# Second layer norm with TensorE's order written down and half its groups made affine ahead of the transpose; another unit order in the second half of the down product; the first norm's first product by parts

## The chip, the cores and the metric

The kernel runs on one core of one Trainium2 chip. The time is the device time of one execution in microseconds; it is given as the median of several runs. The engines are TensorE (PE, with its weight loads PEld), VectorE (DVE), ScalarE (ACT), GpSimd (POOL) and SyncE (SP), which here only issues transfers.

## What is computed

One decoder block on 256 tokens of width 2048, in float32:

```python
x = layer_norm(ALPHA * x + mix, ln1_g[i], ln1_b[i])       # mix: two token mixers, gated, times w_out
ffn = conv_gated_mlp(x, w_gate[i], w_up[i], conv_w[i], conv_b[i], w_down[i])   # 2048 -> 5632 -> 2048
x = layer_norm(ALPHA * x + ffn, ln2_g[i], ln2_b[i])
x = x + jax.nn.sigmoid(x @ w_ple_gate[i]) * (p[i] @ w_ple_proj[i])
```

The stages of the program, in order of time, are the mixers with their projections, the product `wo` with `w_out`, the first layer norm, the gate and up products (44 column groups), the down product in two halves of 1024 output columns, the second layer norm, and the last product `pg` with `w_ple_gate`, whose sigmoid is multiplied with the small projection `pp`.

## The kernel before

**Weights.** Nearly all weights come as units of 128 x 2048 numbers (1 MB), in the order in which they are used. `prep` (L133) fetches a unit in two transfers `raw` from SP's queue and splits it: ScalarE writes the rounded part `hi` (`copy`, L83), VectorE the rest `lo` (L146). A product is then hi x hi + lo x hi + hi x lo. `unit` takes the next unit and prepares up to two ahead. There are four buffers for `raw` and six each for `hi` and `lo`. SP's order is the program's.

**Down product.** Each half (`down`, from L1086) goes over 22 pairs of 128-row groups, one unit a pair, in the order `DN_ORDER`. Fifteen pairs are classic: 24 matmuls, two tiles each of `hi` and `lo`. Seven pairs (`DN_S`) are done with Strassen's seven products: 21 matmuls, but VectorE forms four differences `T` (L127) and splits six tiles (L107, L121). After the last Strassen pair `fold` adds the products up in `z`. The second half holds its last two pairs back as a tail: for each token half `t` and each 512 columns `c` their 12 matmuls are done, and `ev` adds the result to `z` and takes the statistics of these 512 columns (L1144, L1145). A token's four groups `g` of 512 columns are the units of the norm.

**Layer norm.** From the statistics VectorE, GpSimd (the power -1/2) and VectorE again make the mean and the scale. In the second norm (`ln_out`, from L762) each group is then normed (g 0 on VectorE, L774; the others on ScalarE, L777), transposed on TensorE into a bank `ptl` (L780; four transposes of 128 x 128), scaled by gain and bias per channel in four operations on ScalarE and VectorE (L787, L789), and split into the parts of `x2T`. The first norm (`ln_steps`, from L795) does its groups 0 and 2 (`AFF_DVE`) otherwise: two VectorE operations of 512 columns norm them and apply gain and bias (L814, L816) ahead of the transpose, and the transposed bank is split at once (`split_T`, L712). Two banks hold turned groups. What the transposed path leaves undone in `z` itself is done later by `affine` (L862, L864), pulled in between units of the product that follows.

**What sets the order.** A scheduler orders each engine's instructions by priority and its own estimate of when they can run. SP is in program order, and in `end1`, after the product `wo`, so is TensorE: there the turns of the first norm stand between the last quarters of `wo`, the projection `pp` (`proj`) and the first three gate and up products (`psg0`, `psu0`, `psg1`). These three are first done for the first token half (`phase0`, 16 small matmuls each) and then for the second (`phase1`, a group at a time). In the second norm the scheduler sets TensorE's order.

Of the kernel before, what the change touches and what calls it, by code (L numbers as in the profile page):

```python
# [19 lines left out]
P = 128  # L20
# [21 lines left out]
DN_ORDER = (0, 1, 2, 3, 4, 5, 7, 6, 8, 10, 9, 13, 11, 12, 16, 14, 19, 15, 17, 18, 20, 21)  # L42
ZN_DVE = (0,)
# [9 lines left out]
def tile_block(ctx: ExitStack, tc: tile.TileContext, wu, wfv, wpp, xT_in, x_in, pT_in, wlr,  # L53
# [38 lines left out]
    for _ in range(9):  # L92
# [6 lines left out]
    dn_s = {dn0 + nh * (NF // 2) + i for nh in range(2) for i, n in enumerate(DN_ORDER)  # L99
            if n in DN_S}  # L100
# [167 lines left out]
    def x_half(name, act, K, evac, pulls=0, head=0, tail=0, mid=None, done=None, end=None,  # L268
               fine=False):
# [13 lines left out]
        us = [unit() for _ in range(head)]  # L283
        for t in range(2):
            for i, w in enumerate(us):
                mm(i, w, (t,))
        for i in range(head, n - tail):
# [14 lines left out]
        for t in range(2):  # L302
            for c in range(2):
                bs = banks[t][c]
                for j, ps in enumerate(bs):
                    for i, w in enumerate(us):
                        mm(n - tail + i, w, (t,), (c,), j)
                    if len(bs) == 1:
                        evac(t, c, ps)
                    else:  # L310
                        evac(t, c, ps[:, 0:256], (256 * j, 256 * j + 256))
            if done is not None:
                done(t)
# [448 lines left out]
    def ln_out(zof, stats, t, act_out, cg, cb, nm, prio):  # L762

        mv = sm.tile([P, 8], F32, tag="mv", name="mv")
        with tc.high_priority(P_STAT):
            nc.vector.bn_aggr(mv[:, 0:2], stats[t])
            nc.vector.tensor_scalar(mv[:, 2:3], mv[:, 1:2], LN_EPS, None, ALU.add)
            nc.gpsimd.tensor_tensor(mv[:, 3:4], mv[:, 2:3], mhalf, ALU.pow)
            nc.vector.tensor_scalar(mv[:, 4:5], mv[:, 0:1], -1.0, mv[:, 3:4], ALU.mult, ALU.mult)
        with tc.high_priority(prio):  # L770
            for g in range(4):
                zc = zof(t, g)
                if g in ZN_DVE:
                    nc.vector.tensor_scalar(zc, zc, mv[:, 0:1], mv[:, 3:4], ALU.subtract,  # L774
                                            ALU.mult)
                else:
                    nc.scalar.activation(zc, zc, AF.Identity, scale=mv[:, 3:4], bias=mv[:, 4:5])  # L777
                pt = mxtile(f"pt{nm}{t}{g}")
                for i in range(4):
                    nc.tensor.transpose(pt[:, i * P:i * P + P], zc[:, i * P:i * P + P], ident)  # L780
                y = t2("lny").rearrange("p (k t) -> p k t", t=P)
                for i in range(4):
                    kt = 4 * g + i
                    gc, bc = chn[:, cg + kt:cg + kt + 1], chn[:, cb + kt:cb + kt + 1]
                    src = pt[:, i * P:i * P + P]
                    if i % 2:
                        nc.scalar.activation(y[:, i, :], src, AF.Identity, scale=gc, bias=bc)  # L787
                    else:
                        nc.vector.tensor_scalar(y[:, i, :], src, gc, bc, ALU.mult, ALU.add)  # L789
                hi = act_out[g][:, :, t * P:t * P + P]  # L790
                copy(hi, y)
                nc.vector.tensor_tensor(act_out[g][:, :, 256 + t * P:256 + t * P + P], y,
                                        hi.bitcast(F32), ALU.subtract)

    def ln_steps(zs, stats, t, act_out, gb_, cg, cb, nm):  # L795


        z = zs[t]
# [10 lines left out]
        def norm(g):  # L809
            e = slice(g * 512, g * 512 + 512)  # L810
            zc = z[:, e]
            with tc.high_priority(P_LN1[t]):
# [8 lines left out]
        def turn(g):  # L821
            zc = z[:, g * 512:g * 512 + 512]
            with tc.high_priority(P_LN1[t]):
# [22 lines left out]
    def residual(name, act, K, zs, stats, mid, done=None, end=None):  # L846

        for nh in range(2):
            def ev(t, c, ps, nh=nh):
                g = 2 * nh + c  # L850
                zc = zs[t][:, g * 512:g * 512 + 512]
                with tc.high_priority(P_STAT):
# [3 lines left out]
                   done=done if nh == 1 else None, end=end if nh == 1 else None)  # L856

    def affine(zof, gb_, after, gs=range(4)):
        for t in range(2):
            for g in gs:  # L860
                zc = zof(t, g)
                nc.vector.tensor_tensor(zc, zc, gb_[0][:, g * 512:g * 512 + 512], ALU.mult)  # L862
# [40 lines left out]

    def mid1():
        for t in range(2):
            nc.sync.dma_start(z1[t], x_in[t])
        gain[0] = load_gain(0)
# [4 lines left out]
    def end1(tail_mm):  # L912
# [3 lines left out]
        with tc.manual_schedule(engines={mybir.EngineType.PE}):  # L916
# [16 lines left out]
            def phase0(i):  # L933
                us.append(unit())
                ps.append(mmtile(("psg0", "psu0", "psg1")[i]))
                w_phase(ps[i], *us[i], x1T, 0, kts)
# [9 lines left out]
            stat0, norm0, turn0 = ln_steps(z1, st1, 0, x1T, gain[0], c_g1, c_b1, "l1")  # L946
            stat1, norm1, turn1 = ln_steps(z1, st1, 1, x1T, gain[0], c_g1, c_b1, "l1")
# [15 lines left out]
            turn0(G[3])  # L963
# [19 lines left out]
    mixers.append(affine(lambda t, g: z1[t][:, g * 512:g * 512 + 512], gain[0], lambda t: nc.gpsimd.dma_start(x1d[t], z1[t]),  # L983
# [95 lines left out]
    def done2(t):  # L1079
        if t == 1:  # L1080
            pb.extend(ple_proj(1, *pq[0]))
        else:
            x2T.extend(s8([P, 4, 512], F32R, name=f"x2T{g}") for g in range(4))
        ln_out(z2of, st2, t, x2T, c_g2, c_b2, "l2", P_LN2[t])

    def down(nh, tail, mid):  # L1086
# [59 lines left out]

        n = len(DN_ORDER)
        for i, pair in enumerate(DN_ORDER[:n - tail]):
# [3 lines left out]
            if pair == DN_S[-1]:  # L1152
                fold()
        us = [unit() for _ in range(tail)]
        for t in range(2):
            for c in range(2):
                for pair, w in zip(DN_ORDER[n - tail:], us):
                    classic(pair, w, (t,), (c,))
                ev(t, c)
            if tail:  # L1160
                done2(t)
# [6 lines left out]
    down(1, 2, {6: lambda: load_z2(1), 11: late_loads, 17: lambda: pq.append(ple_prep(1))})  # L1168
# [4 lines left out]
    mixers.append(affine(z2of, gain[1], lambda t: None))  # L1173
# [7 lines left out]
    for nh in range(2):  # L1181
# [12 lines left out]
        x_half(f"pg{nh}", x2T, 16, ev_o, pulls=3, head=2 if nh == 0 else 0,  # L1194
# [21 lines left out]
def _dst(w):  # L1216

    out = []
    for nh in range(2):
        for n in DN_ORDER:  # L1220
# [76 lines left out]
```

## Time and profile before

| | us |
|---|---|
| median of 3 runs (lowest, highest) | 1709.33 (1708.78, 1711.75) |
| the profiled execution, its own time | 1707.28 |
| its span | 1705.4 |
| TensorE busy | 1691.5 |
| VectorE busy | 1174.7 |
| ScalarE busy | 862.5 |
| TensorE idle within 857 to 873 (first norm) | 1.05 + 1.65 |
| TensorE idle within 1594 to 1598 (second norm) | 3.14 |

In the rows of the profile an instruction has its line in the kernel, its engine, what it writes and reads by the program's names, and shapes (partitions x columns). "Idle before" is how long the engine did nothing just before, and what ended that. A stretch of time is given in us from the span's start. The granted clock is the share of TensorE's full clock. A matmul's row is longer than its distance from the next, since matmuls overlap.

### The profile page before, as it was taken

The numbers are of one execution on the slowest core, as the hardware profiler recorded it, in microseconds if no ns is written. First come the engines' busy times: TensorE is split into PE (matmuls) and PEld (weight loads), VectorE is DVE, ScalarE is ACT, GpSimd is POOL, SyncE is SP. The second block draws the span as 40 slices with busy tenths as digits, with TensorE's granted clock in tenths as the row PEclk, the third lists the DMA queues.
The fourth block names the chain that finished last, engine by engine and source line by source line (L and its number), as shares of the span: only waits on it lengthen the run. The fifth ranks groups of instructions, "written<-read, shape, count | busy, mean of one in ns | idle before, by whom it ended". The sixth has DMA issues, their size and how long they took to land.

```text
span 1705.4 us, 24004 instructions
## 1 busy us (share of the span) xinstructions
PE 1691.5 (99%) x8993; PEld 1447.4 (85%) x8993; DVE 1174.7 (69%) x1751; ACT 862.5 (51%) x1265; POOL 39.4 (2%) x123
## 2 busy tenths in 40 slices
PE   9999999999999999999999999999999999999998
PEld 8888888888888888888788888888888877878787
DVE  6666658658756557774687677666666887877864
ACT  5745445445555544443365555444444555455633
POOL 0000000000000000000010000000000000000000
PEclk9999999999999999999999999999999999999999
DMA  9654455555555555557665555555555555567454
GB/s 313 229 188 166 164 185 174 177 178 175 174 176 170 168 189 187 189 191 277 214 207 201 186 191 191 186 187 190 192 186 188 171 199 195 197 210 277 162 180 166
DMA packets 91717, 330.24 MB, mean 194 GB/s; under 512 B 10264, under 2 KB 11936, under 8 KB 90448
## 3 DMA queue, kind: packets, MB, share of 16 engines
q1 hardware_dynamic: 90816, 324.51, 56.2%
q0 software_dynamic: 784, 4.20, 0.7%
q8 instruction: 70, 1.15, 0.3%
q14 instruction: 47, 0.39, 0.1%
HBM read 323.42 MB, written 5.25 MB: 193 GB/s over the span
## 4 chain that ended last, share of the span: by engine, by line
PE 93%; DVE 3%; DMA 2%; ACT 1%; issue 1%; SPq 0%; POOL 0%; ACTq 0%; DVEq 0%
PE dn L1106 10%; PE psu L210 9%; PE psg L210 9%; PE psm L210 7%; PE gr L254 5%; PE gv L254 5%; PE psu L212 5%; PE psg L212 5%; PE pg L254 4%; PE psm L212 4%; PE psa L210 3%; PE wo L254 3%; PE fv L361 2%; PE dn_p L1106 2%; DMA raw<-in_wu_dram 2%; PE psa L212 2%
## 5 line engine op out<-in xcount | busy, mean ns | idle before, releaser
L146 DVE TENSOR_TENSOR lo<-raw,hi 128x1024 fp32r<-128x1024 f32 x540 | 658.1, 1223 | 407.0 <-ACT hi L83 405.8
L83 ACT ACTIVATE hi<-raw 128x1024 fp32r<-128x1024 f32 x554 | 585.6, 1059 | 644.4 <-issue 253.2
L210 PE MATMUL psu<-x1T,hi 128*128 128x512 f32 x688 | 242.2, 394 | 0.0
L210 PE MATMUL psg<-x1T,hi 128*128 128x512 f32 x672 | 236.5, 393 | 0.0
L212 PE MATMUL psu<-x1T,lo 128*128 128x256 f32 x688 | 192.6, 280 | 0.0
L212 PE MATMUL psg<-x1T,lo 128*128 128x256 f32 x672 | 188.1, 280 | 0.0
L210 PE MATMUL psm<-xT,hi 128*128 128x512 f32 x512 | 180.1, 395 | 0.0
L210 PEld LDWEIGHTS psu<-x1T,hi 128*128 128x128 f32 x688 | 129.4, 188 | 29.5
L210 PEld LDWEIGHTS psg<-x1T,hi 128*128 128x128 f32 x672 | 126.4, 188 | 28.9
L212 PE MATMUL psm<-xT,lo 128*128 128x256 f32 x512 | 143.3, 280 | 0.0
L1106 PE MATMUL dn<-hi,hC 128*128 128x512 f32 x480 | 135.8, 397 | 0.0
L212 PEld LDWEIGHTS psu<-x1T,lo 128*128 128x128 f32 x688 | 129.4, 188 | 0.0
L212 PEld LDWEIGHTS psg<-x1T,lo 128*128 128x128 f32 x672 | 126.4, 188 | 0.0
L210 PEld LDWEIGHTS psm<-xT,hi 128*128 128x128 f32 x512 | 96.2, 188 | 21.6
L1106 PEld LDWEIGHTS dn<-hi,hC 128*128 128x128 f32 x480 | 90.9, 189 | 21.5
L212 PEld LDWEIGHTS psm<-xT,lo 128*128 128x128 f32 x512 | 96.5, 188 | 0.2
L210 PE MATMUL psa<-oT,hi 128*128 128x512 f32 x256 | 90.1, 393 | 0.0
L1106 PE MATMUL dn<-lo,hC 128*128 128x512 f32 x240 | 77.8, 400 | 0.0
L254 PE MATMUL gv<-hi,xT 128*128 128x512 f32 x256 | 73.6, 399 | 0.0
L254 PE MATMUL gr<-hi,xT 128*128 128x512 f32 x256 | 73.4, 399 | 0.0
L254 PE MATMUL wo<-hi,mT 128*128 128x512 f32 x256 | 71.9, 395 | 0.1
L212 PE MATMUL psa<-oT,lo 128*128 128x256 f32 x256 | 71.6, 280 | 0.0
(500 smaller groups left out, 2745.2 us busy)
## 6 DMA issues: line engine op xcount, KB each, us to landing
raw<-in_wu_dram SPq DMA_DIRECT2D x568, 512.0 KB, 3.6
fvraw<-in_wfv_dram SPq DMA_DIRECT2D x14, 524.0 KB, 6.2
lnb<-in_lng_dram SPq DMA_DIRECT2D x4, 1024.0 KB, 12.1
z<-in_x_dram SPq DMA_DIRECT2D x2, 1024.0 KB, 9.8
praw<-in_wpp_dram SPq DMA_DIRECT2D x4, 512.0 KB, 4.9
x1d<-z POOLq DMA_DIRECT2D x2, 1024.0 KB, 4.9
z<-x1d SPq DMA_DIRECT2D x4, 512.0 KB, 7.6
xraw<-in_xT_dram SPq DMA_DIRECT2D x7, 256.0 KB, 6.8
```

What stands on the lines that cost most here:

```text
L83: nc.scalar.activation(o, i, AF.Copy, bias=0.0, scale=scale)
L146: nc.vector.tensor_tensor(lo, raw, hi.bitcast(F32), ALU.subtract)
L210: nc.tensor.matmul(ps, lhsT=hi[i // 8 if hoff == 0 else 0][:, w0 % 1024:w0 % 1024 + P], rhs=a[:, kt % 4, :], start=first and i == 0, stop= ...
L212: nc.tensor.matmul(ps[:, 256:512], lhsT=lo[i // 8 if hoff == 0 else 0][:, w0 % 1024:w0 % 1024 + P], rhs=a[:, kt % 4, 0:256], start=False, ...
L254: nc.tensor.matmul(bs[j][:, 0:m], lhsT=x, rhs=v[:, o:o + m], start=first and i == 0, stop=last and i == 2)
L361: nc.tensor.matmul(fbk[t][c][:, 0:n], lhsT=x, rhs=w[:, o:o + n], start=kt == 0 and i == 0, stop=kt == 15 and i == 2)
L1106: nc.tensor.matmul(ps, lhsT=x, rhs=w, start=todo[id(ps)] == total[id(ps)], stop=todo[id(ps)] == 1)
```

## The change

It has three parts.

The second norm uses `ln_steps` too, with its groups 0 and 2 made affine ahead of the transpose, and `ln_out` goes. A function `end2` writes down TensorE's order from the tail of the down product to the projection, and `begin2` that of the first four units of `pg`; the turns of the later groups stand between those units. Gain and bias operations left over for `z` are half as many, keep their program order on VectorE in both norms, and are pulled two instead of three a unit.

The second half of the down product gets its own order: Strassen and classic pairs alternate from the second to the fourteenth, and eight classics end it. The loads of `z2`, gain and bias, and projection weights move to earlier units.

In the first norm the last turn of the first token half comes after half of the second token's projection. `phase0` is done in two parts: for three groups of channels in all three products, with a turn of the second token half behind each, and for the fourth group after that.

```diff
-DN_ORDER = (0, 1, 2, 3, 4, 5, 7, 6, 8, 10, 9, 13, 11, 12, 16, 14, 19, 15, 17, 18, 20, 21)
-ZN_DVE = (0,)
+DN_ORDER = ((0, 1, 2, 3, 4, 5, 7, 6, 8, 10, 9, 13, 11, 12, 16, 14, 19, 15, 17, 18, 20, 21),
+            (0, 1, 2, 4, 3, 7, 5, 10, 6, 13, 8, 16, 9, 19, 11, 12, 14, 15, 17, 18, 20, 21))
...
     def affine(zof, gb_, after, gs=range(4)):
         for t in range(2):
             for g in gs:
                 zc = zof(t, g)
-                nc.vector.tensor_tensor(zc, zc, gb_[0][:, g * 512:g * 512 + 512], ALU.mult)
-                yield
-                nc.vector.tensor_tensor(zc, zc, gb_[1][:, g * 512:g * 512 + 512], ALU.add)
-                yield
+                for b, op in zip(gb_, (ALU.mult, ALU.add)):
+                    tc.keep_in_program_order(nc.vector.tensor_tensor(
+                        zc, zc, b[:, g * 512:g * 512 + 512], op))
+                    yield
             after(t)
...
             proj(0, 0)
             turn0(G[2])
             proj(1, 0)
-            turn0(G[3])
             put(0)
             for g in G[:2]:
                 norm1(g)
             proj(0, 1)
+            turn0(G[3])
             proj(1, 1)
             put(1)
-            phase0(0)
-            phase0(1)
-            turn1(G[0])
-            for g in G[2:]:
-                norm1(g)
-            phase0(2)
+            for i in range(3):
+                phase0(i, slice(0, 12))
+                turn1(G[i])
+                if i == 0:
+                    for g in G[2:]:
+                        norm1(g)
+            for i in range(3):
+                phase0(i, slice(12, 16))
             for j in range(4):
-                if j < 3:
-                    turn1(G[j + 1])
                 phase1(j)
+                if j == 0:
+                    turn1(G[3])
...
+    def end2(tail_mm):
+        x2T.extend(s8([P, 4, 512], F32R, name=f"x2T{g}") for g in range(4))
+        w, pTs = pq[0]
+        with tc.manual_schedule(engines={mybir.EngineType.PE}):
+            for c in range(2):
+                for i in range(2):
+                    tail_mm(0, c, i)
...
+            stat0()
+            for g in range(4):
+                norm0(g)
+            for i in range(2):
+                tail_mm(1, 0, i)
+            tail_mm(1, 1, 0)
+            turn0(0)
+            tail_mm(1, 1, 1)
+            stat1()
+            for g in range(4):
+                norm1(g)
+            pb.extend([[mmtile(f"pp1{t}{c}")] for c in range(2)] for t in range(2))
+            for k, t in ((0, 0), (1, 0), (0, 1), (1, 1)):
+                o = slice(k * 1024, k * 1024 + 1024)
+                x_mm(pb, (w[0][:, o], w[1][:, o]), pTs[k], (t,), k == 0, k == 1)
+                if (k, t) == (1, 0):
+                    turn0(1)
+            turn1(0)
+
+    def begin2(mm):
+        with tc.manual_schedule(engines={mybir.EngineType.PE}):
+            us = [unit() for _ in range(2)]
+            for t in range(2):
+                for i in range(2):
+                    mm(i, us[i], (t,))
+                    if t == 0 and i == 0:
+                        turns[1](1)
+            for i in range(2, 4):
+                w = unit()
+                for t in range(2):
+                    mm(i, w, (t,))
+                    turns[t](i)
+                    pull(1)
+        return 4
...
-    down(1, 2, {6: lambda: load_z2(1), 11: late_loads, 17: lambda: pq.append(ple_prep(1))})
+    down(1, 2, {4: lambda: load_z2(1), 8: late_loads, 13: lambda: pq.append(ple_prep(1))})
...
-    mixers.append(affine(z2of, gain[1], lambda t: None))
+    mixers.append(affine(z2of, gain[1], lambda t: None,
+                         [g for g in range(4) if g not in AFF_DVE]))
```

TensorE at the end of the down product before (`dn1_10` and `dn1_11` are the second token's two tail quarters, 12 matmuls each; `ptl200` and `ptl201` the first token's groups 0 and 1 being turned):

```order
L1106 MATMUL dn1_10_13793<-lo267_1_14650,hC7_12639 128x512
L1106 MATMUL dn1_10_13793<-hi267_1_14648,hC7_12639 128x512
L780 MATMUL ptl200_14738<-ident_98,z20_13218 128x128 x4
L780 MATMUL ptl201_14751<-ident_98,z20_13218 128x128 x4
L1106 MATMUL dn1_11_13794<-hi266_0_14606,hC6_12000 128x512
L1106 MATMUL dn1_11_13794<-lo266_0_14608,hC6_12000 128x512
```

and now:

```order
L1065 MATMUL dn1_11_13794<-hi266_1_14612,hC6_12000 128x512
L1065 MATMUL dn1_11_13794<-lo266_1_14614,hC6_12000 128x512
L1065 MATMUL dn1_11_13794<-hi266_1_14612,hC6_12000 128x512
L785 MATMUL ptl200_14766<-ident_98,z20_13218 128x128 x4
L1065 MATMUL dn1_11_13794<-hi267_0_14642,hC7_12639 128x512
L1065 MATMUL dn1_11_13794<-lo267_0_14644,hC7_12639 128x512
```

The first turn stands six matmuls later, with the second turn after the other half of the last quarter and 12 of `pp`.

VectorE at the same place before (`dn1_00` and `dn1_01` are the first token's tail quarters, `lo268` the split of the first unit of `pg`):

```order
L146 TENSOR_TENSOR lo268_0_14680<-raw268_0_14676,hi268_0_14678 128x1024
L146 TENSOR_TENSOR lo268_1_14686<-raw268_1_14682,hi268_1_14684 128x1024
L1144 TENSOR_TENSOR z21_14090<-z21_14090,dn1_00_13791 128x512
L1145 BN_STATS st20_12821<-z21_14090 128x6
L1144 TENSOR_TENSOR z21_14090<-z21_14090,dn1_01_13792 128x512
L1145 BN_STATS st20_12821<-z21_14090 128x6
L766 BN_AGGR mv_14732<-st20_12821 128x2
L767 TENSOR_SCALAR mv_14732<-mv_14732 128x1
L769 TENSOR_SCALAR mv_14732<-mv_14732 128x1
L774 TENSOR_SCALAR z20_13218<-z20_13218,mv_14732 128x512
```

and now:

```order
L1103 TENSOR_TENSOR z21_14021<-z21_14021,dn1_01_13792 128x512
L1104 BN_STATS st20_12821<-z21_14021 128x6
L762 BN_AGGR mv_14734<-st20_12821 128x2
L763 TENSOR_SCALAR mv_14734<-mv_14734 128x1
L773 SCALAR_TENSOR_TENSOR z20_13218<-z20_13218,mv_14734,lnb10_14210 128x512
L765 TENSOR_SCALAR mv_14734<-mv_14734 128x1
L773 SCALAR_TENSOR_TENSOR z21_14021<-z21_14021,mv_14734,lnb10_14210 128x512
L1103 TENSOR_TENSOR z21_14021<-z21_14021,dn1_10_13793 128x512
L775 SCALAR_TENSOR_TENSOR z20_13218<-z20_13218,mv_14734,lnb11_14211 128x512
```

The splits of `lo268` still stand ahead of the first sum; between the scale and the first group that can be turned there are now an affine step and a sum more.

VectorE after the first norm's last split for the first token, before (`lo137` and `lo138` are split weights, `ptl111` the first turn of the second token, L862 and L864 the late gain and bias):

```order
L146 TENSOR_TENSOR lo137_1_7759<-raw137_1_7755,hi137_1_7757 128x1024
L146 TENSOR_TENSOR lo138_0_7920<-raw138_0_7916,hi138_0_7918 128x1024
L146 TENSOR_TENSOR lo138_1_7926<-raw138_1_7922,hi138_1_7924 128x1024
L862 TENSOR_TENSOR z10_7186<-z10_7186,lnb00_7380 128x512
L838 TENSOR_SCALAR lny_7979<-ptl111_7974,chn_97 128x128
L864 TENSOR_TENSOR z10_7186<-z10_7186,lnb01_7381 128x512
L838 TENSOR_SCALAR lny_7979<-ptl111_7974,chn_97 128x128
L862 TENSOR_TENSOR z10_7186<-z10_7186,lnb00_7380 128x512
L862 TENSOR_TENSOR z11_7187<-z11_7187,lnb00_7380 128x512
L841 TENSOR_TENSOR x1T1_7191<-lny_7979,x1T1_7191 128x4x128
```

and now:

```order
L146 TENSOR_TENSOR lo137_1_7759<-raw137_1_7755,hi137_1_7757 128x1024
L797 TENSOR_SCALAR lny_7946<-ptl111_7941,chn_97 128x128
L146 TENSOR_TENSOR lo138_0_7920<-raw138_0_7916,hi138_0_7918 128x1024
L797 TENSOR_SCALAR lny_7946<-ptl111_7941,chn_97 128x128
L705 TENSOR_TENSOR x1T0_7190<-ptl110_7981,x1T0_7190 128x4x128
L146 TENSOR_TENSOR lo138_1_7926<-raw138_1_7922,hi138_1_7924 128x1024
L800 TENSOR_TENSOR x1T1_7191<-lny_7946,x1T1_7191 128x4x128
```

The gain and bias operations are gone from here (they now come between later gate and up products), and the split of the turned group 0 comes ahead of group 1's. The rows of VectorE ahead of this place are the same in both kernels.

More of the change, by code (lines that the diff above doesn't have):

```diff
@@ L266, in pull, with x_half @@
                     mixers.pop(0)
[L268 to L269 removed]
+    def x_half(name, act, K, evac, pulls=0, begin=None, tail=0, mid=None, end=None, fine=False):
         banks = [[[mmtile(f"{name}_{t}{c}")] for c in range(2)] for t in range(2)]
@@ L281, in mm @@
                      kt == 0, kt == K - 1, cs, part)
[L283 to L287, printed above, removed]
+        for i in range(begin(mm) if begin else 0, n - tail):
             mm(i, unit(), (0, 1))
@@ L760, in tile_block, with ln_steps @@
     ppd = dr.tile([2, P, 1024], F32, name="ppd")
[L762 to L798, printed above, removed]
+    def ln_steps(zof, stats, t, act_out, gb_, cg, cb, nm, prio):
         mv = sm.tile([P, 8], F32, tag="mv", name="mv")
@@ L1151, in down, with tail_mm @@
                 mid[i]()
-            if pair == DN_S[-1]:
+            if not set(DN_ORDER[nh][i:]) & set(DN_S) - {pair} and pair in DN_S:
                 fold()
         us = [unit() for _ in range(tail)]
+        def tail_mm(t, c, i):
+            classic(DN_ORDER[nh][n - tail + i], us[i], (t,), (c,))
+            if i == tail - 1:
+                ev(t, c)
+        if tail:
+            end2(tail_mm)
+            return
         for t in range(2):
             for c in range(2):
-                for pair, w in zip(DN_ORDER[n - tail:], us):
-                    classic(pair, w, (t,), (c,))
```

57 lines of the change are left out of this document (28 added, 29 removed).

## The prediction

> **What bounds the kernel now.** I read the busy line of the page first, then busy time by stage, then the list of what TensorE waited for, then the stretches around those waits. The page has engine, busy us, share of the span, instructions; a stage row has the stretch, its length, busy us of PE, PEld, DVE, ACT and POOL, the granted TensorE clock, the DMA share and GB/s.
>
> ```profile
> PE 1691.5 (99%) x8993; PEld 1447.4 (85%) x8993; DVE 1174.7 (69%) x1751; ACT 862.5 (51%) x1265; POOL 39.4 (2%) x123
> 920.00:1340.00 420.00, 420.00 (x2409) 368.23 (x2408) 288.21 (x418) 205.32 (x295) 14.12 (x76) 1.00 0.56 189
> 1340.00:1577.00 237.00, 236.96 (x1043) 190.87 (x1042) 189.11 (x262) 125.13 (x167) 0.81 (x4) 1.00 0.61 209
> ```
>
> TensorE is never idle in the gate and up products (920 to 1340) nor in most of the down product (1340 to 1577). The number of matmuls doesn't change, so only its gaps can be won, 1705.4 - 1691.5 = 13.9 us in all. Of those in the middle of the program, the list of waits (waiter, releaser: us in total, times, longest) names three that the change touches:
>
> ```profile
> PE ptl L780 <- DVE z L774: 3.1, 1, 3.1
> PE psg L223 <- DVE x1T L841: 1.7, 1, 1.7
> PE ptl L826 <- DVE x1T L712: 1.1, 1, 1.1
> 857.00:863.00 6.00, 4.95 (x26) 3.71 (x25) 5.93 (x13) 6.00 (x11) 1.70 (x3) 1.00 0.38 132
> 868.00:873.00 5.00, 3.35 (x29) 3.11 (x28) 5.00 (x10) 2.03 (x4) 0.00 (x0) 1.00 0.94 288
> 1594.00:1598.00 4.00, 0.86 (x8) 0.72 (x8) 3.06 (x9) 1.19 (x2) 0.56 (x1) 1.00 0.57 183
> 1598.00:1602.00 4.00, 4.00 (x14) 3.19 (x13) 3.65 (x7) 3.82 (x8) 0.00 (x0) 0.57 0.00 0
> ```
>
> The first norm costs 1.1 + 1.7 us of waiting; VectorE is busy all through both stretches (5.93 of 6, 5.00 of 5), so it is what TensorE waits for. The second norm costs 3.1 us of waiting, and then 4 us at a clock of 0.57, in which 4 x (1 - 0.57) = 1.7 us are lost without any idle time. After the shorter waits the clock stayed at 1.00. What the change could win is thus at most some 2.8 + 3.1 + 1.7, or about 8 us with the matmuls' tails (below).
>
> **First norm by parts.** Rows of the timeline (start us, us, engine, line, what):
>
> ```profile
> 857.84 1.63 PE L254 MATMUL pp<-pw,pTs 128*128 128x512 f32 x6
> 859.79 0.68 DVE L712 TENSOR_TENSOR x1T<-ptl,x1T 128x512 fp32r<-128x512 f32 x1
> 860.52 0.66 PE L826 MATMUL ptl<-ident,z 128*128 128x128 f32 x4 [1.05 <-DVE x1T L712]
> 860.94 3.02 PE L254 MATMUL pp<-pw,pTs 128*128 128x512 f32 x12
> 863.79 2.23 PE L223 MATMUL psg<-x1T,hi 128*128 128x256 f32 x16
> 863.95 0.68 DVE L841 TENSOR_TENSOR x1T<-lny,x1T 128x512 fp32r<-128x512 f32 x1
> 865.15 3.48 DVE L146 TENSOR_TENSOR lo<-raw,hi 128x1024 fp32r<-128x1024 f32 x3
> 865.86 2.06 PE L223 MATMUL psu<-x1T,hi 128*128 128x256 f32 x16
> 867.76 0.60 PE L826 MATMUL ptl<-ident,z 128*128 128x128 f32 x4
> 868.56 0.68 DVE L862 TENSOR_TENSOR z<-z,lnb 128x512 f32<-128x512 f32 x1
> 869.16 0.40 DVE L838 TENSOR_SCALAR lny<-ptl,chn 128x128 f32<-128x128 f32 x1
> 870.10 0.60 PE L826 MATMUL ptl<-ident,z 128*128 128x128 f32 x4
> 872.35 0.39 PE L223 MATMUL psg<-x1T,hi 128*128 128x256 f32 x1 [1.65 <-DVE x1T L841]
> ```
>
> A pp matmul takes (863.79 - 860.94) / 12 = 0.237 us start to start, a small psu one (867.76 - 865.86) / 16 = 0.119, a turn of four transposes 860.94 - 860.52 = 0.42. The last turn of the first token is put six pp later: TensorE comes to it at 857.84 + 12 x 0.237 = 860.7, when its bank has just been read (859.79 + 0.68 = 860.5). That wait is gone; the turn and the six other pp end at 862.5, and eight small matmuls of the first part at 863.5. The next four need the third group, which VectorE finishes at 863.95 + 0.68 = 864.6, and VectorE's rows up to there are the same in both kernels. So TensorE waits 1.1 us there instead: in this half nothing is won, the wait moves.
>
> The second wait is different. From 864.7 on there are 40 small matmuls (4.8 us) and now three turns instead of two. By the old rows the second turn ends at 870.5, so with a third the second token's products can begin at 870.9. Their data come from VectorE, where four gain and bias operations of the first norm no longer stand ahead: from 865.15 three weight splits of 1.16, two scalings of 0.40 and two x1T splits of 0.68 end at 870.8. So they start at 870.9 instead of 872.35, with one turn more done: 1.45 + 0.42 = **1.9 us won**. Bounds: 3.0 if both waits vanish, 0.7 if one more weight split (1.16) gets ahead.
>
> **Second norm.**
>
> ```profile
> 1589.08 1.06 ACT L83 ACTIVATE hi<-raw 128x1024 fp32r<-128x1024 f32 x1 [2.55 <-DMA raw<-in_wu_dram]
> 1590.18 2.57 DVE L146 TENSOR_TENSOR lo<-raw,hi 128x1024 fp32r<-128x1024 f32 x2 [2.39 <-ACT hi L83]
> 1592.67 0.68 DVE L1144 TENSOR_TENSOR z<-z,dn 128x512 f32<-128x512 f32 x1
> 1593.74 0.40 PE L1106 MATMUL dn<-hi,hC 128*128 128x512 f32 x1
> 1593.99 0.67 DVE L1144 TENSOR_TENSOR z<-z,dn 128x512 f32<-128x512 f32 x1
> 1596.56 0.21 DVE L769 TENSOR_SCALAR mv<-mv 128x1 f32<-128x1 f32 x1 [0.68 <-POOL mv L768]
> 1597.28 1.09 PE L780 MATMUL ptl<-ident,z 128*128 128x128 f32 x8 [3.14 <-DVE z L774]
> 849.56 0.69 DVE L853 SCALAR_TENSOR_TENSOR z<-z,wo 128x512 f32<-128x512 f32 x1 [1.38 <-PE wo L254]
> 852.56 0.22 DVE L806 TENSOR_SCALAR mv<-mv 128x1 f32<-128x1 f32 x1 [0.44 <-POOL mv L805]
> 852.69 0.74 DVE L816 SCALAR_TENSOR_TENSOR z<-z,mv,lnb 128x512 f32<-128x512 f32 x1
> 1359.60 5.57 PE dn L1106 x24
> ```
>
> The last row is from the chain of waits: 24 down matmuls in 5.57 us, 0.232 each. TensorE ended three of the four tail quarters (12 matmuls, 2.8 us each) at 1593.97, so the first token's last quarter at 1591.2. Its sums began only at 1592.67 and 1593.99: VectorE stood behind the splits of the first weights of the last product, which waited for ScalarE, which waited for their DMA. Then TensorE had eight transposes in its queue with 12 matmuls of the last quarter behind them.
>
> Now 18 matmuls stand ahead of the first transposes: TensorE comes to them at 1591.2 + 18 x 0.232 = 1595.4. Eight classic units come last in the second half, and the projection's weights are fetched four units earlier, so the splits need no late DMA: the one that was late needs a buffer that TensorE frees when the tail begins (1593.97 - 3 x 2.8 = 1585.6), and is then done in 1.06 + 1.22 us, at 1587.9, before the first quarter ends at 1588.4. So the chain starts at 1591.2 plus the 0.2 that the last matmul takes to land. From the second sum to the scale factor it took 1596.56 - 1593.99 = 2.6 us here and 852.56 - 849.56 = 3.0 in the first norm: 1594.0 to 1594.4. Then VectorE has 0.2, one affine step (0.74), one sum (0.68) and the second affine step (0.74), less 0.07 of overlap each: 1596.1 to 1596.6. TensorE waits 0.7 to 1.2, say 0.9. For the second token 24 pp, two turns and six matmuls (8 us) cover a like chain that has two weight splits more; I put 0.3 there. Lost before: 1597.28 - 1593.97 = 3.3 and 1.7 of slow clock, 5.0 in all; lost now: 1.2; **won 3.8 us**. Bounds: 5.0 if no wait is left, -0.1 if VectorE is as late as before (3.4 of waiting and the same clock).
>
> Half the groups are now made affine on VectorE, eight steps of 0.74; three for each token stand ahead of its first transposes and are in the chain above. What this saves, 16 scalings of turned groups (half on ScalarE, 0.40 each on VectorE) and eight of 16 late gain and bias operations, lies beside TensorE's work in the last product, where VectorE isn't full: I cost it at nothing. If that cover were gone, the eight steps would be 5.9 us against the 8 x 0.40 and 8 x 0.68 saved, 8.6: no loss.
>
> **Other unit order in the second half.** Strassen and classic units alternate seven times where they had gaps of two classics.
>
> ```profile
> DVE T L127 <- DMA raw<-in_wu_dram: 14.9, 11, 3.9
> PEld dn L1106 <- DVE lo L146: 2.0, 6, 0.4
> DMA to landing us min/median/max: 3.5/5.3/8.3
> 1553.09 1.89 DVE L107 TENSOR_TENSOR T_260l<-T,T_260h 128x512 fp32r<-128x512 f32 x3
> ```
>
> A pair takes TensorE 21 + 24 matmuls, 45 x 0.232 = 10.4 us, and VectorE nine operations of 1.89 / 3 = 0.63 and three of 1.16, 9.2 us: 88%, no bound by itself. The tight loop is through the four weight buffers: a Strassen unit's second half is fetched only when the unit of its kind before has been read to the end (landing 5.3), and then five operations of 0.63 and two of 1.16 follow until the next can be asked for, 5.5: 10.8 us against 10.4. Each pair falls 0.4 behind, 2.4 over six; how far the splits are ahead when it begins I estimate at 3 us, half a classic unit (5.57), since the six buffers of split weights hold one Strassen unit or three classics. I take 0.2 lost; bounds 0.3 won (the waits of PEld above) and, with 8.3 for every landing, 3.4 x 6 - 3 = 17 lost.
>
> **Sum.** 1.9 + 3.8 - 0.2 = 5.5. The profiled execution took 1707.28 (span 1705.4), 2.05 below the median 1709.33. 1707.28 - 5.5 = 1701.8, and as a median **1703.8 us**.
>
> **The rivals.** *VectorE stays late in the second norm* (its wait for weights is behind the 3.1 us; against it the classics and the earlier fetch): 1.6 won, 1707.7. *The first norm's waits only move* (VectorE is full there, and the first of them does move): 1705.7. *The buffers starve TensorE in the second half*, the side of slower: place, the alternating units; price, landing + 5.5 - 10.4 for each of six pairs after the first 3 us; for it 14.9 us of VectorE waiting for weights, against it that TensorE lost next to nothing where one such pair stood. It decides from a mean landing of 6.9 (2.0 x 6 - 3 = 9 lost, 3.5 more than is won); at 7.5 it is 12.6 lost, 1716. *Everything fits*: 8.0 won, 1701.1. [...] *The written order isn't kept* is all but excluded by the rows of the order: 1709.
>
> **Numbers.** Forecast 0.55 (its own range 1702.3 to 1705.5), VectorE late 0.13, first norm nothing 0.10, starving 0.09, everything 0.06, clock 0.04, order not kept 0.03. Changes within 0.2%, 3.4 us, can't be told from none. Faster by more (below 1705.9): nearly all of the forecast, all of the case in which everything fits, half of the cases at 1705.5 and 1705.7: 0.68. Slower: most of starving, 0.08. The rest, 0.24. The range 1701.0 to 1709.3 leaves out the starving case and the edges of the best one.
>
> **What would show it.** Right: no wait of TensorE over 1.3 us in either norm, a granted clock near 1.00 after the second, the first wait in the first norm now before the third group's small matmuls, VectorE's sums of the first token within 0.5 us of TensorE's quarters, and no new wait from 1480 to 1580. Wrong: the sums behind weight splits again; rows of PE waiting for T or lo in the alternating units; waits on ScalarE's table load or splits after the first norm.

## The result, and the profile after

The changed kernel takes 1709.36 us (median of 12 runs, 1706.58 to 1714.81) against 1710.41 for the kernel before on the same chip (12 runs): a ratio of 0.9988 [0.9979, 0.9998]. It is 0.12% faster, about 2 us (0.3 to 3.6 by the interval); 5.5 were forecast.

The waits of TensorE in the changed kernel (waiter, releaser: us in total, times, longest):

```profile
PE dn L1065 <- DVE T_228l L107: 1.6, 1, 1.6
PE dn L1065 <- DVE T_247l L107: 1.5, 1, 1.5
...
PE psg L223 <- DVE x1T L800: 1.1, 1, 1.1
PE ptl L785 <- DVE z L775: 1.1, 1, 1.1
PE dn L1065 <- DVE lo L121: 0.9, 1, 0.9
PE dn L1065 <- DVE lo L146: 0.8, 2, 0.6
...
PE dn L1065 <- DVE T_249l L107: 0.6, 1, 0.6
```

Each norm is down to one wait of 1.1 us. What was not there before are the rows of `dn`: T_247l, T_249l and `lo` belong to the alternating units. In the second half's stretch (columns as in the prediction's stage rows) TensorE was busy all of the 102 us before, the first row; now, the second, it is not:

```profile
1475.00:1577.00 102.00, 102.00 (x438) 81.50 (x437) 79.04 (x101) 52.42 (x67) 0.00 (x0) 1.00 0.64 223
1475.00:1577.00 102.00, 98.03 (x413) 76.50 (x412) 80.88 (x107) 52.40 (x67) 0.00 (x0) 1.00 0.64 217
```

To set the stages against each other I worked out for every kernel, from the matmuls of its profile, how far the distances from one start to the next exceed the usual one of their shape (0.2325 us for 512 columns, 0.1175 for 256, and so on). The sums follow the spans of all kernels here to 0.1 us. The limits are 850, 1340, 1478 and 1580 us, so that "first norm" also holds what follows the norm in the gate and up products, and "all" is the whole program. Small negative values come from the usual distance being rounded. Each row is a single execution, and not always a typical one: that of e2 was the fastest of its five runs, that of e6 the slowest of its ten.

| us lost in | before 850 | first norm | first half | second half | second norm | all |
|---|---|---|---|---|---|---|
| before | 10.4 | 2.9 | 0.8 | 0.7 | 5.4 | 20.3 |
| changed | 10.6 | 1.4 | 2.4 | 6.3 | 1.5 | 22.5 |
| e1 old units, old places | 10.4 | 1.4 | 1.7 | 2.5 | 6.2 | 22.5 |
| e2 old units, new places | 10.3 | 1.4 | 1.9 | 1.1 | 1.5 | 16.5 |
| e3 new units, old places | 11.8 | 1.4 | 2.1 | 10.4 | 1.3 | 27.4 |
| e4 before + units, places | 9.6 | 2.9 | 1.8 | 8.0 | 1.0 | 23.6 |
| e5 changed, VectorE's order held | 11.1 | 1.4 | 1.6 | 1.2 | 1.5 | 17.1 |
| e6 e2, held in both halves | 12.7 | 1.4 | 4.7 | 4.1 | 1.5 | 24.9 |
| e7 before + places | 10.9 | 3.0 | 1.9 | 4.7 | 1.2 | 21.7 |
| e8 e2, only projection moved | 9.8 | 1.4 | 1.4 | 2.6 | 5.2 | 20.7 |
| e9 e5, held from unit 228 | 10.9 | 1.4 | -0.2 | 0.8 | 1.5 | 14.7 |
| e10 e4, held | 10.0 | 3.0 | 1.6 | -0.1 | 1.2 | 15.8 |
| e11 e10 + first norm | 10.9 | 1.4 | 0.9 | 1.6 | 1.2 | 16.1 |
| e12 e9, gain later | 12.5 | 1.4 | -0.1 | 0.0 | 2.3 | 16.3 |

The table closes: from before to changed 1.5 and 3.9 are won, 5.6 and 1.6 lost and 0.4 is spread over the start and the end, in all 2.2 more; the two profiled executions differ by 1709.36 - 1707.28 = 2.1. I count the 1.6 of the first half, where the code is the same, as no part of the change: the old program loses 0.8 to 1.9 there (before, e4, e7, e10), so the profiled execution of before lies at the low end. It also lay 3.1 us below the median of its 12 runs, so the table may make every other kernel look somewhat worse against before than the medians do.

### The profile page after: what moved, and what is told of

Read it like the earlier page. It is cut to its first block, busy times and chain, and to the rows that moved or that the text cites. A ratio compares the mean times of both kernels' runs of the same rounds, so it can differ in the third digit from the quotient of the medians.

```text
span 1707.5 us, 23977 instructions
## 1 busy us (share of the span) xinstructions
PE 1692.7 (99%) x8993; PEld 1447.4 (85%) x8993; DVE 1172.5 (69%) x1741; ACT 859.2 (50%) x1255; POOL 36.2 (2%) x123
## 4 chain that ended last, share of the span: by engine, by line
PE 89%; DMA 5%; DVE 4%; issue 1%; ACT 1%; SPq 0%; POOL 0%; ACTq 0%; DVEq 0%
PE psu L210 9%; PE psg L210 9%; PE psm L210 7%; PE dn L1065 6%; PE gv L254 5%; PE gr L254 5%; PE pg L254 5%; PE psu L212 5%; PE psg L212 5%; DMA raw<-in_wu_dram 4%; PE psm L212 4%; PE psa L210 3%; PE wo L254 3%; PE fv L354 2%; PE psa L212 2%; PE psfq L210 2%
```

## Why the second half lost time

VectorE's rows at the start of the alternating units, changed kernel (start, us, engine, line; idle before, releaser in brackets):

```profile
1480.42 0.69 DVE L127 TENSOR_TENSOR T<-raw 128x512 f32<-128x512 f32 x1 [4.36 <-DMA raw<-in_wu_dram]
1481.03 0.69 DVE L107 TENSOR_TENSOR T_247l<-T,T_247h 128x512 fp32r<-128x512 f32 x1
1481.63 2.47 DVE L1103 TENSOR_TENSOR z<-z,dn 128x512 f32<-128x512 f32 x4
1484.02 2.47 DVE L1104 BATCH_NORM_STATS2 st<-z 128x6 f32<-128x512 f32 x4
1486.41 1.28 DVE L107 TENSOR_TENSOR T_247l<-T,T_247h 128x512 fp32r<-128x512 f32 x2
1487.60 0.68 DVE L127 TENSOR_TENSOR T<-raw,raw 128x512 f32<-128x512 f32 x1
1488.20 1.41 DVE L127 TENSOR_TENSOR T<-raw,T 128x512 f32<-128x512 f32 x2
1489.53 0.68 DVE L107 TENSOR_TENSOR T_247l<-T,T_247h 128x512 fp32r<-128x512 f32 x1
```

The profile's rows leave unit numbers out of `T<-raw`; the written order has them. It puts `T1_249<-raw249_0` ahead of `T1_247l`, the eight sums and statistics of the first half, `T3_247l` and `T2_247l`, and `T3_249`, `T2_249` and `T4_249` ahead of `T4_247l`. So VectorE stands 4.36 us before a difference of unit **249**, whose weights are on their way, while the splits of unit **247**, which TensorE multiplies next, are behind it. ScalarE had the first of their rounded parts ready at 1476.6, soon after VectorE began to wait, and the last at 1484.9; TensorE came to the last split 1.48 us too early:

```profile
1475.94 0.64 ACT L83 ACTIVATE T_247h<-T 128x512 fp32r<-128x512 f32 x1 [1.75 <-PE dn L1065]
...
1484.31 0.63 ACT L83 ACTIVATE T_247h<-T 128x512 fp32r<-128x512 f32 x1 [2.15 <-PE dn L1065]
1488.40 0.39 PE L1065 MATMUL dn<-T_247h,hS 128*128 128x512 f32 x1
1490.27 0.50 PE L1065 MATMUL dn<-T_247l,hS 128*128 128x512 f32 x1 [1.48 <-DVE T_247l L107]
```

VectorE began that last split at 1489.53. Between 1475 and 1580 VectorE stands four times before a difference whose weights are under way, in the changed kernel:

```profile
DVE T L127 <- DMA raw<-in_wu_dram: 16.1, 4, 4.4
```

In the kernel before the same row reads

```profile
DVE T L127 <- DMA raw<-in_wu_dram: 12.5, 9, 3.9
```

so it waits there too, but TensorE lost next to nothing by it. What counts is what stands behind.

In the old order unit 249 is classic, the next difference belongs to unit 250, and nothing of it stands ahead of unit 247's splits.

## The experiments

All ratios are to the kernel before, run on the same chip in the same session (29 runs beside e1 to e4 with a median of 1711.28, 31 beside e5 to e8 with 1709.91, 11 beside e9 to e12 with 1711.05).

**e1 to e3: the unit order and the places of the loads, each put back.** e1 changes both lines, e2 the first, e3 the second:

```diff
-            (0, 1, 2, 4, 3, 7, 5, 10, 6, 13, 8, 16, 9, 19, 11, 12, 14, 15, 17, 18, 20, 21))
+            (0, 1, 2, 3, 4, 5, 7, 6, 8, 10, 9, 13, 11, 12, 16, 14, 19, 15, 17, 18, 20, 21))
...
-    down(1, 2, {4: lambda: load_z2(1), 8: late_loads, 13: lambda: pq.append(ple_prep(1))})
+    down(1, 2, {6: lambda: load_z2(1), 11: late_loads, 17: lambda: pq.append(ple_prep(1))})
```

> The changed kernel, with the second half of the down product back in the old unit order and its three sets of loads back at the old units; both norms stay changed. Theory A (the alternating units lose what the norms win, because weights come late in them): the waits for T and lo between 1490 and 1560 go, and the kernel is 4 to 5 us faster than the changed one, near 1705 (0.997 of before). Theory B (the loads of z2, gain and projection weights among these units are what makes the weights late): the same time here, since both go back. Theory C (the norms win less than their waits show): within 1 us of the changed kernel, near 1709. Rival D (the eight classics at the end are what brings the second norm in time): the alternating waits go, but the second norm waits 3 us again, near 1708.

Measured: 1709.99 us, 0.9993 [0.9985, 1.0002]. The rival D came: the second half's loss falls (6.3 to 2.5 in the table; one wait of 1.2 us, for T_255l, stays), but the second norm, in its new program, is at least as late as before the change, and the clock falls after it:

```profile
PE ptl L785 <- DVE z L775: 3.8, 1, 3.8
1602.00:1604.00 2.00, 2.00 (x7) 1.51 (x6) 1.56 (x3) 2.00 (x4) 0.00 (x0) 0.51 0.00 0
```

> The changed kernel with only the unit order of the second half put back; the loads of z2, gain and projection weights stay at the new units (positions 4, 8 and 13). Theory A (the order itself): as fast as with both put back, near 1705. Theory B (the loads among the units): near 1709, with waits of TensorE within 10 us after the loads. Theory C: near 1709 whatever the order.

Measured: 1705.54 us, 0.9967 [0.9955, 0.9979]. Theory A's number. Both norms have their one wait of 1.1, and the second half loses 1.1 in all. So in this execution the new places cost little in the old order (0.4 more than before), and theory B in its simple form is out; e7 below, with the same order and places, lost more.

> The changed kernel with only the three sets of loads put back to positions 6, 11 and 17; the new unit order stays. Theory A (the order itself): no gain against the changed kernel, near 1709, waits for T and lo between 1490 and 1560 as before. Theory B (the loads): near 1705, without these waits. Later loads may make the second norm wait up to 1 us more in both.

Measured: 1712.81 us, 1.0009 [0.9998, 1.0021]. Theory B is refuted: with the loads back the alternating units lose 10.4, more than in the changed kernel, 3.1 of it in one wait for `lo` behind differences that waited for transfers, and about 1.7 in the slow clock that followed (granted clock 0.70, 0.50 and 0.94 in the three stretches of 2 us from 1552 on). The second norm, in its new program, is in time here (1.3), with the old places: the new order brings it there too.

**e4: the kernel before with the order and the places, and nothing else.** The diff is the table `DN_ORDER` and the line of `down` from the change.

> The kernel before with nothing but the new unit order of the second half and the new places of the three sets of loads. Theory A: 4 to 5 us of waits for T and lo in the alternating units, against at most 3.3 + 1.7 us won in the second norm if the classics at the end bring it in time by themselves: between 1710 and 1715. Theory C: the order costs at most 0.5, so 1709 to 1711 with the second norm as late as before, or near 1706 if the classics help it. Rival D (the classics at the end are what repairs the second norm): no wait above 1.3 us at the first turn of the second norm, although its program is the old one.

Measured: 1710.84 us, 0.9999 [0.9989, 1.0008]. Theory A's loss (8.0 in the second half) and rival D's repair: the old program of the second norm has no long wait any more.

```profile
PE dn L1108 <- DVE T_247l L109: 1.5, 1, 1.5
...
PE ptl L782 <- DVE z L776: 0.6, 1, 0.6
```

**e5: the changed kernel with VectorE's order held in the alternating units.** Each weight operation is kept behind what the program puts before it on VectorE:

```diff
+    def pin(u, ins):
+        if dn0 + 22 <= u < dn0 + 37:
+            tc.keep_in_program_order(ins)
...
-            nc.vector.tensor_tensor(ts[n], a, ts.get(b, b) if isinstance(b, str) else b,
-                                    ALU.subtract)
+            pin(u, nc.vector.tensor_tensor(ts[n], a, ts.get(b, b) if isinstance(b, str) else b,
+                                           ALU.subtract))
...
-            nc.vector.tensor_tensor(lo, raw, hi.bitcast(F32), ALU.subtract)
+            pin(u, nc.vector.tensor_tensor(lo, raw, hi.bitcast(F32), ALU.subtract))
```

> The changed kernel with one thing more: in the alternating units VectorE's weight operations (differences T, their splits, lo) are held to the program's order, so that no difference of the next Strassen unit, which waits for its transfer, stands ahead of the last splits of the unit before. Theory E (VectorE's own order: ready splits queue behind a difference that waits for a transfer): the waits for T_247l (1.5 us) and T_249l (0.6) go and most of those for lo with them, 2 to 4 us faster than the changed kernel, near 1706. Theory F (the loop through the four weight buffers is too slow, whatever the order): the waits only move to other tiles of the same units, within 1 us of the changed kernel, near 1709.

Measured: 1704.07 us, 0.9968 [0.9957, 0.9978]: theory E. Against the changed kernel that is 0.0020 of 1710, 3.4 us (about 1.0 to 5.8, the two half-widths added in squares). VectorE's rows at the same place, and the stage:

```profile
1475.08 0.69 DVE L127 TENSOR_TENSOR T<-raw 128x512 f32<-128x512 f32 x1
...
1476.89 2.58 DVE L1107 TENSOR_TENSOR z<-z,dn 128x512 f32<-128x512 f32 x4
1479.39 2.46 DVE L1108 BATCH_NORM_STATS2 st<-z 128x6 f32<-128x512 f32 x4
...
1482.36 1.89 DVE L107 TENSOR_TENSOR T_247l<-T,T_247h 128x512 fp32r<-128x512 f32 x3
1484.70 0.69 DVE L107 TENSOR_TENSOR T_247l<-T,T_247h 128x512 fp32r<-128x512 f32 x1 [0.45 <-ACT T_247h L83]
1475.00:1577.00 102.00, 101.73 (x435) 81.12 (x434) 86.15 (x113) 55.26 (x70) 0.00 (x0) 1.00 0.66 228
```

The last split of unit 247 starts at 1484.70 instead of 1489.53, waiting for ScalarE alone, and TensorE has 3.7 us more of work in the stage. All five kernels with the alternating order held lose -0.1 to 1.6 in this stage, the three with it not held 6.3 to 10.4. Theory F, my prediction's rival of the starved buffers, is out. VectorE still waits in e5, up to 3.5 us at a time for ScalarE's rounding, but no longer ahead of a split that TensorE needs first.

**e6: the same in both halves, old unit order.** The condition of `pin` becomes `dn0 <= u < dn0 + 41`, in the kernel of e2.

> The kernel of e2 (both norms changed, old unit order, loads at the new units) with VectorE's weight operations held to the program's order in both halves of the down product. Theory E: the wait for T_228l in the first half (1.0 to 1.6 us in every run of a kernel with these norms) goes, since the differences of unit 230 no longer stand ahead of the last split of unit 228: 1 to 1.5 us faster than e2, near 1704.3. Theory F: T_228l stays late or another tile of that unit is, the same time as e2, 1705.5.

Measured: 1709.61 us, 0.9998 [0.9988, 1.0008], some 5 us slower than e2 by the ratios. T_228l's wait is gone as theory E said, but another of 3.0 us takes its place: held from the first unit on, the split of unit 226 comes behind the sums that prepare the Strassen products, which the scheduler could move and now can't. After it, too, the clock falls:

```profile
PE dn L1069 <- DVE lo L150: 3.0, 1, 3.0
1376.00:1378.00 2.00, 2.00 (x6) 1.60 (x5) 2.00 (x2) 0.00 (x0) 0.00 (x0) 0.50 0.74 233
```

In the second half it also loses 4.1. There VectorE, in the program's order, stands for long before the split of a unit's second half, which waits for ScalarE's rounding:

```profile
DVE lo L121 <- ACT hi L83: 13.6, 6, 3.4
```

So holding the order doesn't help as such. My reading is that it helps where the program's order is also the order of arrival; e6 alone doesn't show that.

**e7: the kernel before with the new places of the loads alone** (the line of `down`).

> The kernel before with nothing but the new places of the three sets of loads (positions 4, 8 and 13 instead of 6, 11 and 17); unit order and both norms as before. Theory G (the earlier loads are what brings the second norm in time): the 3.1 us wait at its first turn falls below 1 us and the slow clock after it is gone, 3.5 to 4.5 us faster than before, near 1707. Theory H (the written order of TensorE and the affine groups are needed for it): a wait of 2 to 3 us stays, within 1 us of before.

Measured: 1706.68 us, 0.9984 [0.9973, 0.9994]. Theory G: the first turn of the second norm waits 0.6, the stage loses 1.2 instead of 5.4, and the old program of the norm did it.

```profile
PE dn L1106 <- ACT T_260h L83: 1.3, 1, 1.3
...
PE ptl L780 <- DVE z L774: 0.6, 1, 0.6
```

By the ratio 2.7 us are won (1.0 to 4.6), less than the 3.5 to 4.5 expected, though the interval reaches there. This execution lost 4.7 in the second half. The first row is a part of it, and behind it the clock fell:

```profile
1558.85 1.06 ACT L83 ACTIVATE pw<-praw 128x1024 fp32r<-128x1024 f32 x1 [1.73 <-DMA praw<-in_wpp_dram]
1560.43 0.61 ACT L83 ACTIVATE T_260h<-T 128x512 fp32r<-128x512 f32 x1
1562.00:1564.00 2.00, 2.00 (x5) 1.54 (x6) 2.00 (x4) 1.46 (x2) 0.00 (x0) 0.50 0.76 215
```

It looks like the same fault on ScalarE: it stands 1.73 us before the projection's weights, now loaded at this place, with the last rounding of T_260 behind them. In the kernel before, that rounding began 3.9 us ahead of the first matmul that uses it (1553.52 and 1557.45), here 0.7 (1561.10), in e2 0.9 (1555.74 and 1556.60). So moving the loads has a price of its own. No run was made to separate it.

**e8: only the projection's weights at the new place** (6, 11 and 13 in the line of `down`, the rest as in e2).

> The kernel of e2 with z2 and the gain and bias rows back at positions 6 and 11; only the projection's weights stay at the new position 13. Theory G1 (of the three sets it is the projection's weights, whose buffers and splits otherwise fall together with the fold just before the tail): as fast as e2, 1705.5, with the second norm's wait near 1.1. Theory G2 (the other loads matter as well): between e2 and e1, 1707 to 1710, with a wait above 2 us at the first turn of the second norm.

Measured: 1705.95 us, 0.9981 [0.9972, 0.9991]. The ratio lies between e2's and e1's, though its interval overlaps both, and the profile has G2's wait, 3.2 us at the first turn, with a clock of 0.50 behind it. The projection alone is not enough; which of the other two matters I didn't separate.

```profile
PE ptl L785 <- DVE z L775: 3.2, 1, 3.2
1600.00:1602.00 2.00, 2.00 (x6) 1.59 (x5) 1.51 (x2) 2.00 (x3) 0.00 (x0) 0.50 0.03 8
```

**e9: e5, held from unit 228 of the first half on, too** (`dn0 + 4 <= u < dn0 + 37`).

> The kernel of e5 with VectorE's weight operations held to the program's order from unit 228 of the first half on, too (in e6 the order was held from the first unit of the down product, and the split of unit 226 came behind the sums for the Strassen products). Theory E (ready splits queue behind a difference that waits for a transfer): T_228l's wait of 1.2 us goes as well and lo of 226 is no later than in e5, so 1.0 to 1.3 us faster than e5, near 1703.0. Theory F: the wait moves to another tile of unit 228 or 230, the same time as e5.

Measured: 1701.57 us (1700.24 to 1702.47), 0.9949 [0.9937, 0.9961]: faster than both kernels, 8.7 us below before. Its list of waits has no row of the down product left:

```profile
PE warm_ps L93 <- DVE warm L90: 1.2, 1, 1.2
PE fv L358 <- ACT fvhi L83: 1.1, 1, 1.1
PE psg L227 <- DVE x1T L804: 1.1, 1, 1.1
PE ptl L789 <- DVE z L779: 1.1, 1, 1.1
PE wo L258 <- DVE z L816: 0.4, 1, 0.4
```

The first half has the same fault wherever the order isn't held, in the kernel before too: three differences of unit 230 stand ahead of the last split of unit 228. More is won than the 1.0 to 1.3 expected (0.0019 of 1710, 3.2 us, with intervals of 2 on each); the stage shows 1.8.

**e10 and e11: e5 without the norms' changes, and with the first norm's alone.** e10 is e4 with the `pin` of e5; e11 adds the change of `end1` and of `affine` for the first norm.

> The kernel before with the new unit order, the new places of the loads and VectorE's weight order of e5, but with both norms as before. Theory I (the second norm is in time through the loads alone, and its rewriting wins nothing): only the first norm's 1.9 us are missing against e5, so near 1706, and at the first turn of the second norm a wait of 0.6 to 0.7 as in e4 and e7. Theory H (the written order and the affine groups win most of what is won in the second norm): 1.9 + 2 to 4 us are missing, 1708 to 1710.

> The kernel of e10 with the first norm's change added, so e5 with only the second norm's program as before. The first norm's term of the prediction says 1.9 us faster than e10. Theory I: the same time as e5 or up to 0.5 faster, near 1704. Theory H: 2 to 4 us slower than e5, near 1707.

Measured: 1704.85 us, 0.9967 [0.9955, 0.9978], and 1703.39 us, 0.9959 [0.9947, 0.9971]. Theory I: with e5 at 0.9968, the second norm's rewriting wins nothing that can be measured; in the table it is 0.3 slower (1.2 in e10 and e11, 1.5 in e5 and e9). The first norm's term is about 1.5 in both the medians and the table (3.0 to 1.4); the times alone wouldn't show it, their intervals overlap.

**e12: e9 with the gain and bias rows at position 14.**

> The kernel of e9 with the gain and bias rows (two transfers of 1 MB each in the chip's memory terms of the tile) fetched at position 14, after the last alternating unit, instead of 8. Theory J (of what is left, the waits for T_257h and T_257l, 0.9 us in e5, come from these transfers standing ahead of a Strassen unit's second half): they go, and the kernel is 0.5 to 1 us faster than e9. Rival: they then stand ahead of the classics' weights or come too late for the second norm, whose first wait grows from 1.1 to 2 us or more: slower than e9 by 1 us or more.

Measured: 1703.29 us, 0.9955 [0.9941, 0.9969]. In e5's list no matmul waits for T_257, only weight loads do. Both theories come true in part: the second half loses nothing at all (0.8 in e9), and the first turn waits 1.8 us instead of 1.1. The median is 1.7 above e9's, but the intervals overlap, and the profiled execution lost 1.6 more at its start as well, a stretch that the edit doesn't touch. No gain over e9 is shown, and no loss either.

## Why the prediction was right or wrong

**That it gets a little faster** was right, but by less than half of what was forecast. On the prediction's base the ratio gives 1709.33 x 0.9988 = 1707.3: inside the wide range, outside the forecast's own 1702.3 to 1705.5, and within the 0.2% that the prediction couldn't tell from none, to which it gave 0.24 against 0.68 for more. That the number lies near the rival *VectorE stays late* (1707.7) is chance: that rival didn't happen. Two of the three terms came as forecast, and the third failed.

**First norm, 1.9 forecast, 1.5 won.** The first wait moved, as said, to the third group's small matmuls, and the second vanished:

```profile
862.66 1.11 PE L223 MATMUL psg<-x1T,hi 128*128 128x256 f32 x8
864.86 0.74 PE L223 MATMUL psg<-x1T,hi 128*128 128x256 f32 x4 [1.09 <-DVE x1T L800]
```

1.1 was forecast, 1.09 measured. Around the norm itself 2.0 is won; 0.5 of it is lost again by 1340, in the products that follow, which I didn't trace. 1.5 remains.

**Second norm, 3.8 forecast, 3.9 won.** The size was right (5.4 to 1.5), and the chain too:

```profile
1597.28 0.69 DVE L1103 TENSOR_TENSOR z<-z,dn 128x512 f32<-128x512 f32 x1 [1.27 <-PE dn L1065]
1600.30 0.22 DVE L765 TENSOR_SCALAR mv<-mv 128x1 f32<-128x1 f32 x1 [0.46 <-POOL mv L764]
1602.49 0.66 PE L785 MATMUL ptl<-ident,z 128*128 128x128 f32 x4 [1.06 <-DVE z L775]
1600.00:1604.00 4.00, 2.94 (x16) 2.14 (x15) 3.70 (x7) 3.45 (x5) 0.26 (x1) 1.00 0.02 4
```

The first sum still comes right behind a weight split, at 1594.60, but the second now waits for TensorE, not for splits; the scale factor follows 3.0 us after the second sum's start (2.6 to 3.0 forecast), the turn waits 1.06 (0.7 to 1.2), and the clock stays at 1.00. What earned it was only half told: the prediction joined the written order, the eight classics and the earlier loads. By e1 the written order and the affine groups alone do nothing for it; by e2 and e7 the new places alone suffice, with the new program or the old, and by e3 the new unit order alone with the new program (with the old one it was tried only together with the places, e4). In e4, e7, e10 and e11 the old program is as quick or quicker. VectorE's lateness came from the weights, and the weights are what had to be moved.

**Other unit order, 0.2 lost: the mis-sized term.** It measures 5.6 in the profiles and 3.4 in the times (e5 against the changed kernel). The step that failed is "five operations of 0.63 and two of 1.16 follow until the next can be asked for, 5.5: 10.8 us against 10.4". It let VectorE's operations run one after another as their inputs came. In the profile VectorE kept to its written order, and that had a difference which waited 4.36 us for a transfer ahead of sums and splits that were ready. With the order held, the loop costs about as little as the sum says: 0.5 in the stage (1.2 in e5 against 0.7 before; -0.8 to 0.9 over the five kernels). The whole kernel e5 is at 0.9968, 5.5 us below before, which is the prediction's sum; with an interval of 2 us each way and a first norm that won 1.5 instead of 1.9, that exact number is partly luck. The sign of the 4.36 us was in the order of the changed kernel's instructions, which I read for the norms and not for these units.

**The rivals.** The starved buffers named the right place and the wrong mechanism: the half lost 5.6, where that rival needed 9 from a mean landing of 6.9. The median landing from 1478 to 1556 was 5.5 us in the changed kernel against 5.4 before; from 1475 to 1545 it was 6.3 and 5.6, and 4.1 in e5, where nothing but VectorE's order was edited. The 1.7 us in the forecast's clock case (1705.5, 0.04) were measured behind the 3.1 us wait of before; no run shows them behind several short ones: in the changed kernel the clock stayed at 1.00 with six of 0.2 to 1.5 us from 1486 to 1556, and e7's one stretch at 0.50, behind waits of 1.3 and 0.23 us, has 1.0.

## What to carry to other kernels

When a change reorders units of different kinds, read the order on every engine that feeds TensorE, and look for an operation that waits for a transfer ahead of operations that are ready: sums of busy time don't show its price (of the 102 us from 1475 to 1577 VectorE was busy 79.0 before, 80.9 in the changed kernel and 86.2 in e5, TensorE 102.0, 98.0 and 101.7). Hold the order there, and only there: held over both halves, in the old unit order, it cost some 5 us (e6). And undo each part by itself before crediting a rewriting: here one line that moves loads won what the rewritten norm seemed to.

## What the runs showed of the hardware that I had not expected

The length of the wait alone doesn't say when the slow clock comes. Each of the five waits of 3.0 to 3.8 us (before, e1, e3, e6, e8) was followed by a granted clock of 0.50 to 0.53 in the slowest stretch of 2 us, wherever it lay, and one of 2.1 us at the start of e12 by 0.54, the list's row and the two stretches behind it:

```profile
PE fv L358 <- ACT fvhi L83: 2.1, 1, 2.1
14.00:16.00 2.00, 1.95 (x8) 1.67 (x7) 1.93 (x3) 1.54 (x4) 0.00 (x0) 0.60 0.94 303
16.00:18.00 2.00, 2.00 (x9) 2.00 (x8) 1.87 (x3) 1.77 (x2) 0.00 (x0) 0.54 0.93 289
```

The slow clock also followed the wait of only 1.3 us in e7, with one of 0.23 us right behind it (the clock of 0.50 shown there). It didn't follow longer waits of 1.8 us: e5 has one at the same place of the program as e12's 2.1 and keeps 1.00, e6 one in `wo` (1.00 from 811 to 817), and e12 itself one in its second norm:

```profile
1596.00:1600.00 4.00, 3.69 (x18) 3.12 (x19) 4.00 (x7) 4.00 (x5) 0.00 (x0) 1.00 0.07 13
```

So all six waits of 2.1 us and more brought the slow clock, and of the shorter ones shown here a single one; what set that one apart is open. Behind each of the six the slow clock cost 1.7 us more than the wait's length (stretch by stretch 2 x (1 - clock): in the kernel before 2 x (0.38 + 0.47), in e12 2 x (0.40 + 0.46)); behind that of e7 the one stretch shown has 2 x 0.50 = 1.0.
